# Weight tiles in a hybrid SSD and RWKV-7 step: four buffers for either part and four raw tiles while the mixer lasts, in a pool of its own

## The chip, the cores and the metric

One core of one Trainium2 chip runs the whole step. The time is device microseconds of one launch, the median of several runs. The profile comes from one profiled execution, whose own time stands beside its span below. Engines are named as in the profile: PE (matrix multiplies; PEld its weight loads), DVE, ACT, POOL, and SP, which issues nearly all DMAs.

## The reference, cut to what matters

One layer of a decoder over 576 tokens: 512 of a prompt and 8 sequences of 8 tokens with states of their own. Everything is float32.

```python
u = rmsnorm(h)
z, xbc, dt_raw, rw = jnp.split(u @ w_in, IN_SPLITS, axis=-1)     # 1024 -> 1024 + 1536 + 16 + 3328
# group A, Mamba-2 SSD, 16 heads x 64, state 128
xs, bm, cm = jnp.split(silu(conv4(xbc)), XBC_SPLITS, axis=-1)
y_ssd = ssd_norm * group_rmsnorm((ssd_chunked(xs, dt, a_head, bm, cm, ssm0) + d_skip * xs) * silu(z))
# group B, RWKV-7, 16 heads x 64
r, k, v, w_lo, a_lo, g_lo = jnp.split(rw + (prev - rw) * shift_mu, RWKV_SPLITS, axis=-1)
decay = exp(-exp(-softplus(-(w0 + tanh(w_lo) @ w2)) - 0.5)); a = sigmoid(a0 + a_lo @ a2)
gate = sigmoid(g_lo) @ g2
# per token: S = S * decay - (S kk)(kk*a)^T + v k^T ; o = S r
y_rwkv = (group_norm(o) * ln_x_w + ln_x_b + bonus) * gate
h += concat(y_ssd, y_rwkv) @ w_out                                # 2048 -> 1024
h += (silu(rmsnorm(h) @ w_gate) * (rmsnorm(h) @ w_up)) @ w_down   # 1024 -> 2816 -> 1024
h += sigmoid(rmsnorm(h) @ w_ple_gate) * (p @ w_ple_proj)
y = rmsnorm(h)
```

## The kernel before, in words

**A projection.** Activations lie channel by token: a tile is 128 channels x 576 tokens, used in two halves of 288. A float32 product is made of rounded parts: a weight block of 128x512 (four 128x128 weights) comes by one DMA of 256 KB into a tile `raw`; ACT copies it rounded into `whi`; POOL and DVE in turn subtract it, `wlo = raw - whi`. `wsplit` does these three steps (L206 the DMA, the helper `act` at L93 the copy, L213 the subtraction). The activations are split alike into `xhi` and `xlo`. For each 128x128 weight and each half `mm3` issues three matmuls: `whi` by `xhi` (L228), `whi` by `xlo` (L229), `wlo` by `xhi` (L230); a 1024-row projection of one 128-channel tile takes two blocks and 48 matmuls. Another order of the same three products, used late in the program, has line L241.

**The pool `wp`.** It lives for the whole program and holds three tiles `raw`, two `whi` and two `wlo`, 2 KB a partition each: 14 KB a partition. A tile's next user waits until the last reader of the one before is done: the DMA for `wlo` on the same `raw`, ACT's copy for the last matmul L229 on the same `whi`, the subtraction for the last matmul L230 on the same `wlo`.

**The mixer** runs until `mix.close()`, at about 680 us. RWKV's heads are worked in four quarters Q0 to Q3, each through these steps: its projections (`shifted`, L368 to L378, with the gate tiles, which need the tile `vo` made at L442 and by `split`); **prep** (L568 to L592, two passes jj0 and jj1: decay products `pb`, normalised keys `kk`, L588 and then POOL's L592, which writes half of `bk`); **gram** (L620 on PE, masked by DVE at L630 into `Lst`); a triangular **solve** on DVE (L681, L683) with round trips through DRAM; **combine** (L705 to L719); a **chain** of nine dependent steps `core` (L796, L804, L809, L819, with `prompt_state` L830 on PE and L838 on DVE); and `head_norm` (L908 on). L253 is a sum over channels behind the gram. The projections that belong to no quarter (`xbc`, `dt` and `z` tiles) are handed out between those steps and fill PE in the waits of a chain: this text calls all projection matmuls L228 to L230 the filler.

**Order.** The program is written as above, but the order on each engine is set when it is built: a scheduler goes through the written instructions with a priority for each, keeps a model of when buffers and engines come free, and puts out one list per engine. Each engine then works its list strictly in order. A change of the buffers of a pool therefore changes the lists.

**After the mixer** come the output projection, SwiGLU and the per-layer embedding, with `h` in the pool `hp` and other pools on the right side of the memory.

Of the kernel before, what the change touches and what calls it, by code (L numbers as in the profile page):

```python
# [8 lines left out]
F32 = mybir.dt.float32  # L9
F32R = mybir.dt.float32r  # L10
AF = mybir.ActivationFunctionType
ALU = mybir.AluOpType
# [4 lines left out]
P = 128  # L17
# [58 lines left out]
def hybrid_step(ctx, tc, A):  # L76
    nc = tc.nc
    V, S, G, T = nc.vector, nc.scalar, nc.gpsimd, nc.tensor

    cp = ctx.enter_context(tc.tile_pool(name="cp", bufs=1))  # L80
    wp = ctx.enter_context(tc.tile_pool(name="wp", bufs=2))
    xp = ctx.enter_context(tc.tile_pool(name="xp", bufs=8))
    lin = ctx.enter_context(tc.tile_pool(name="lin", bufs=2, space=PSUM))
    dp = ctx.enter_context(tc.tile_pool(name="dp", bufs=1, space=DRAM))
# [3 lines left out]
    def nm(s):  # L88
        uid[0] += 1
        return f"{s}_{uid[0]}"  # L90

    def act(out, in_, func=AF.Copy, scale=1.0, bias=0.0):
        return S.activation(out, in_, func, bias=bias, scale=scale)  # L93
# [80 lines left out]
    at, n = PV["shift_mu"]  # L174
    V.tensor_scalar(omu[:], pv[:, at:at + n], -1.0, 1.0, ALU.mult, ALU.add)
    hka = const("hka", [P, 16])
    at, n = PV["k_a"]
# [4 lines left out]
    flip = [0]  # L182
    only = [None]

    def below(lo, src, hi, eng):

        if eng == "D":
            act(lo, src, scale=-1.0)
            G.dma_start(lo, src, accum_op=ALU.add)
        else:  # L190
            eng.tensor_tensor(lo, src, hi.bitcast(F32), ALU.subtract)  # L191

    def split(src, pool, tags, shape, lo_eng=None, hi=None, lo=None, hi_eng=None, **kw):
# [7 lines left out]
        below(lo[:], src, hi[:], lo_eng or (G if flip[0] % 2 else V))  # L201
        return hi, lo

    def wsplit(src, n, hi=None, lo=None):
        raw = wp.tile([P, 512], F32, tag="raw", name=nm("raw"), bufs=3)
        nc.sync.dma_start(raw[:, 0:n], src)  # L206
        if hi is None:
            hi = wp.tile([P, 512], F32R, tag="whi", name=nm("whi"))
            lo = wp.tile([P, 512], F32R, tag="wlo", name=nm("wlo"))
        act(hi[:, 0:n], raw[:, 0:n])  # L210
        flip[0] += 1
        eng = only[0] or (G if flip[0] % 2 else V)
        eng.tensor_tensor(lo[:, 0:n], raw[:, 0:n], hi[:, 0:n].bitcast(F32), ALU.subtract)  # L213
        return hi, lo

    ahead = []
# [1 line left out]
    def wload(nk, hi=None, lo=None):  # L218
        if ahead:
            return ahead.pop(0)  # L220
        n = nk * P
        src = A["wts"][wat[0]:wat[0] + P * n].rearrange("(p n) -> p n", p=P)
        wat[0] += P * n
        return wsplit(src, n, hi, lo)
# [29 lines left out]


    mix = ExitStack()
    sp = mix.enter_context(tc.tile_pool(name="sp", bufs=1, side="right"))
    s2_ = ExitStack()
    s2 = s2_.enter_context(tc.tile_pool(name="s2", bufs=1, side="right"))
# [48 lines left out]
    for k in range(KT):  # L308
        hi, lo = xu[0][:, k], xu[1][:, k]
# [111 lines left out]
    def dts():  # L421
        hi, lo = wsplit(A["wdt"], P)
        ps = lin_ps()[0:16]
        for k in range(KT):
            mm3(ps, hi[:, k * 16:k * 16 + 16], lo[:, k * 16:k * 16 + 16], X[k][0], X[k][1], k == 0, k == KT - 1)
        x = cslot("dtx", [16, NT])
        act(x[:], ps, AF.Identity, bias=sm16[:, 0:1])
        e = cslot("dte", [16, NT])
        V.scalar_tensor_tensor(e[:], x[:], -1.0, x[:], ALU.mult, ALU.max)
        act(e[:], e[:], AF.Exp, scale=-1.0)  # L430
        act(e[:], e[:], AF.Ln, bias=1.0)
        V.scalar_tensor_tensor(x[:], x[:], 0.0, e[:], ALU.max, ALU.add)
        nc.sync.dma_start(dt_d[:], x[:])
# [11 lines left out]
    def gates(ugh):  # L445
        for h in range(2):
            gh, gl = wsplit(A["wg2"][:, h * 512:h * 512 + 512], 512)
            for jj in range(4):
                ps = lin_ps()
                mm3(ps, gh[:, jj * P:(jj + 1) * P], gl[:, jj * P:(jj + 1) * P], ugh[0], ugh[1], True, True)  # L450
                g = slot("g")
                act(g[:], ps)
                nc.sync.dma_start(gate_d[h * 4 + jj][:], g[:])
# [431 lines left out]
    def gate_bonus(j):  # L885
        if j < 6 and j % 2 == 0:
            gt, y = (sp.tile([P, NT], F32, tag="gt", name=nm(n), bufs=2)[:] for n in ("gt", "bvl"))
        else:
            t = pair(j // 2, "gb")
            gt, y = t[:, 0], t[:, 1]  # L890
        nc.sync.dma_start(gt, gate_d[j][:])
        nc.sync.dma_start(y, bv_d[j][:])
        return gt, y

    def head_norm(s, ahead=()):

        q = s.q
        st = tr_ps()[:, 0:20]
        Oc = []
        gsq = None if ahead else pair(q, "gsq")  # L900
        if not ahead:
            ahead = [gate_bonus(2 * q), gate_bonus(2 * q + 1)]
        for jj in jj2:
            o = s.AR[:, jj].rearrange("p g t -> p (g t)")
            sq = gsq[:, jj] if gsq else sp.tile([P, NT], F32, tag="gt", name=nm("gsq"), bufs=2)
            for a, b in HV:
                pp = cx_ps()
                marks["n", q] = T.matmul(pp[:, 0:HALF], cen[:], o[:, a:b], start=True, stop=True)  # L908
                V.tensor_copy(o[:, a:b], pp[:, 0:HALF])
                act(sq[:, a:b], pp[:, 0:HALF], AF.Square)  # L910
            token_sums(st, jj, sq)
            Oc.append(o)
        rn = inv_norm(st, "gnr", 1.0 / 64, GN_EPS)
        for jj in jj2:
            j = 2 * q + jj
            o = Oc[jj]
            gt, y = ahead[jj]
            for a, b, ps in by_channel(rn, jj, cx_ps, "rxg"):
                V.scalar_tensor_tensor(o[:, a:b], o[:, a:b], par("ln_x_w", j), ps, ALU.mult, ALU.mult)
            (V if q == 3 else G).tensor_tensor(y, y, o, ALU.add)  # L920
            yo = sp.tile([P, NT], F32, tag="gt", name=nm("yo"), bufs=2)[:] if q == 2 and jj else y
            V.scalar_tensor_tensor(yo, y, par("ln_x_b", j), gt, ALU.add, ALU.mult)
            if q < 3:
                nc.sync.dma_start(yr_d[j][:], yo)
            else:
                YR.append(split(y, xp, ("xhi", "xlo"), [P, NT], lo_eng=V))
# [357 lines left out]
    with tc.high_priority():  # L1284
        head_norm(Q[3], [gate_bonus(6), gate_bonus(7)])
    mix.close()
    hp = ctx.enter_context(tc.tile_pool(name="hp", bufs=8, side="right", reuse_waits="tile"))
    late.append(mix2.enter_context(tc.tile_pool(name="mz", bufs=1, side="right", reuse_waits="tile")))
    late.append(mix2.enter_context(tc.tile_pool(name="ps2", bufs=1, space=PSUM, reuse_waits="tile")))
# [244 lines left out]
    for a, b in ((0, 320), (320, NT)):  # L1534
        n = b - a
# [17 lines left out]
        for c in range(8):  # L1553
# [6 lines left out]
            for k in range(KT):  # L1560
                hi, lo = (w[:, k % 4 * P:k % 4 * P + P] for w in WP[c][k // 4])
# [166 lines left out]
```

## Time and profile before

| | |
|---|---|
| median of 3 runs | 1332.21 us (1329.48, 1332.21, 1340.11) |
| the profiled execution | 1330.78 us, span 1328.8 us, clock granted to PE 0.95 |
| PE / PEld | 1225.6 us (92%) / 1127.1 us (85%) |
| DVE | 887.1 us (67%) |
| ACT | 631.1 us (47%) |
| POOL | 611.6 us (46%) |
| DMA | 140.29 MB, mean 106 GB/s |

The profile's page counts each engine's busy time over the span. Its queries group instructions by line, list what each engine waited for, cut the span into windows, and print instructions one by one with the idle time ahead of them and what ended it. In a window's row stand the bounds, the length, then the busy time of PE, PEld, DVE, ACT and POOL with the number of instructions, the granted clock (PEclk, 1.00 is full), the share of DMA time and GB/s. In a row of waits stand the waiting engine, line and tile, what released it, the sum in us, the number of times and the longest. In a timeline row stand start, duration, engine, line, operation, and in brackets the idle time before it and its releaser.

### The profile page before, as it was taken

The numbers are of one execution on the slowest core, as the hardware profiler recorded it, in microseconds if no ns is written. First come the engines' busy times: TensorE is split into PE (matmuls) and PEld (weight loads), VectorE is DVE, ScalarE is ACT, GpSimd is POOL, SyncE is SP. The second block draws the span as 40 slices with busy tenths as digits, with TensorE's granted clock in tenths as the row PEclk, the third lists the DMA queues.
The fourth block names the chain that finished last, engine by engine and source line by source line (L and its number), as shares of the span: only waits on it lengthen the run. The fifth ranks groups of instructions, "written<-read, shape, count | busy, mean of one in ns | idle before, by whom it ended". The sixth has DMA issues, their size and how long they took to land. (4 is left out here: it accounts for less than half of the span.)

```text
span 1328.8 us, 26626 instructions
## 1 busy us (share of the span) xinstructions
PE 1225.6 (92%) x10429; PEld 1127.1 (85%) x10429; DVE 887.1 (67%) x1570; ACT 631.1 (47%) x1274; POOL 611.6 (46%) x583
## 2 busy tenths in 40 slices
PE   6897999999989978899989988999999999999997
PEld 5786897889968966787869868899899999999996
DVE  6648666887696886953456567868895148883464
ACT  6565436534654373343434464455553225553363
POOL 5416513642365135122455655646465345655642
PEclk9898899899978979889989989999999999999998
DMA  5322242234232313262454542253333224424322
GB/s 166 122 69 72 78 116 67 86 96 121 72 110 74 100 52 87 95 200 88 140 187 140 176 151 65 72 169 106 96 107 89 87 76 114 125 57 135 100 88 72
DMA packets 96765, 140.29 MB, mean 106 GB/s; under 512 B 34961, under 2 KB 39313, under 8 KB 96641
## 3 DMA queue, kind: packets, MB, share of 16 engines
q1 hardware_dynamic: 93760, 133.36, 32.8%
q0 software_dynamic: 2304, 4.72, 2.0%
q8 instruction: 82, 1.34, 0.4%
q10 hardware_dynamic: 576, 0.52, 0.1%
q14 instruction: 43, 0.34, 0.1%
HBM read 106.10 MB, written 27.75 MB: 101 GB/s over the span
## 5 line engine op out<-in xcount | busy, mean ns | idle before, releaser
L213 POOL TENSOR_TENSOR wlo<-raw,whi 128x512 fp32r<-128x512 f32 (+1 forms) x92 | 125.4, 1363 | 307.9 <-ACT whi L93 230.3
L228 PE MATMUL lin<-xhi,whi 128*128 128x288 f32 (+1 forms) x784 | 243.0, 311 | 2.9 <-ACT whi L93 2.1
L230 PE MATMUL lin<-xhi,wlo 128*128 128x288 f32 (+1 forms) x784 | 241.2, 308 | 2.2 <-POOL wlo L213 2.2
L229 PE MATMUL lin<-xlo,whi 128*128 128x288 f32 (+1 forms) x784 | 240.8, 307 | 0.9 <-POOL xlo L191 0.9
L93 ACT ACTIVATE whi<-raw 128x512 fp32r<-128x512 f32 (+1 forms) x200 | 123.2, 616 | 213.3 <-PE lin L241 94.9
L228 PEld LDWEIGHTS lin<-xhi,whi 128*128 128x128 f32 (+1 forms) x784 | 150.5, 192 | 9.8 <-ACT whi L93 2.6
L229 PEld LDWEIGHTS lin<-xlo,whi 128*128 128x128 f32 (+1 forms) x784 | 150.3, 192 | 6.2 <-POOL xlo L191 2.1
L230 PEld LDWEIGHTS lin<-xhi,wlo 128*128 128x128 f32 (+1 forms) x784 | 150.3, 192 | 6.0 <-POOL wlo L213 2.8
L213 DVE TENSOR_TENSOR wlo<-raw,whi 128x512 fp32r<-128x512 f32 (+1 forms) x108 | 83.5, 774 | 73.5 <-PE lin L241 37.7
L1424 PE MATMUL lin<-T,wh 128*128 128x288 f32 x576 | 87.3, 296 | 2.6 <-ACT e L93 2.2
L1424 PEld LDWEIGHTS lin<-T,wh 128*128 128x128 f32 x576 | 80.2, 190 | 3.3 <-ACT e L93 2.4
L93 ACT ACTIVATE wh<-raw 128x512 fp32r<-128x512 f32 x72 | 45.1, 629 | 53.9 <-PE lin L1424 37.1
L191 POOL TENSOR_TENSOR wl<-raw,wh 128x512 fp32r<-128x512 f32 x36 | 57.1, 1586 | 13.1 <-PE lin L1424 7.5
L191 DVE TENSOR_TENSOR wl<-sw,wh 128x512 fp32r<-128x512 f32 x54 | 50.8, 940 | 8.6 <-ACT wh L93 4.5
L241 PE MATMUL lin<-ah,whi 128*128 128x288 f32 x352 | 54.7, 294 | 0.0
L241 PE MATMUL lin<-al,whi 128*128 128x288 f32 x352 | 54.4, 295 | 0.0
L241 PE MATMUL lin<-ah,wlo 128*128 128x288 f32 x352 | 54.2, 295 | 0.0
L681 DVE TENSOR_TENSOR tmp<-L,Tt 72x30 f32<-72x30 f32 (+14 forms) x120 | 51.4, 429 | 3.2
L1424 PE MATMUL lin<-T,wl 128*128 128x288 f32 x288 | 50.2, 299 | 0.0
L241 PEld LDWEIGHTS lin<-ah,whi 128*128 128x128 f32 x352 | 49.3, 188 | 0.0
L241 PEld LDWEIGHTS lin<-al,whi 128*128 128x128 f32 x352 | 49.2, 188 | 0.0
L241 PEld LDWEIGHTS lin<-ah,wlo 128*128 128x128 f32 x352 | 49.2, 188 | 0.0
(432 smaller groups left out, 3259.2 us busy)
## 6 DMA issues: line engine op xcount, KB each, us to landing
raw<-wts SPq DMA_DIRECT2D x271, 256.0 KB, 2.6
S<-s_wkv SPq DMA_DIRECT2D x8, 512.0 KB, 5.1
hd<-s_ssm SPq DMA_DIRECT2D x8, 512.0 KB, 3.5
o_ssm_s<-hd SPq DMA_DIRECT2D x8, 512.0 KB, 2.9
xbc_d<-E SPq DMA_DIRECT2D x12, 288.0 KB, 2.1
x<-xT SPq DMA_DIRECT2D x8, 288.0 KB
gate_d<-g SPq DMA_DIRECT2D x8, 288.0 KB, 2.5
bv_d<-rw SPq DMA_DIRECT2D x8, 288.0 KB
```

Source lines behind the costliest of these rows:

```text
L93: return S.activation(out, in_, func, bias=bias, scale=scale)
L191: eng.tensor_tensor(lo, src, hi.bitcast(F32), ALU.subtract)
L213: eng.tensor_tensor(lo[:, 0:n], raw[:, 0:n], hi[:, 0:n].bitcast(F32), ALU.subtract)
L228: T.matmul(ps[:, a:b], whi, xhi[:, a:b], start=first, stop=False)
L229: T.matmul(ps[:, a:b], whi, xlo[:, a:b], start=False, stop=False)
L230: T.matmul(ps[:, a:b], wlo, xhi[:, a:b], start=False, stop=last)
L241: T.matmul(ps[:, a:e], (hi, lo)[p][:, i * P:(i + 1) * P], xs[k + i][q][:, a:e], start=n == k + i == 0, stop=n == 2 and k + i == nk - 1, sk ...
L681: V.tensor_tensor(o, L[:, jx:jx + 1, jx + 1:32].to_broadcast([NB, jx, n]), Tt[:, 0:jx, jx:jx + 1].to_broadcast([NB, jx, n]), ALU.mult)
L1424: T.matmul(ps, (hi, lo)[p][:, k * P:(k + 1) * P], OPS[n][k][q], start=first and p == q == k == 0, stop=p == 1 and k == 3, skip_group_check ...
```

## The change

`wp` is no longer opened at the start. A pool `wm` on the right side, inside the stack `mix`, serves the weight blocks until `mix.close()`, with four `raw`, four `whi` and four `wlo`: 24 KB a partition. Behind `mix.close()` a new `wp` is opened on the right side with the old numbers, three `raw` and two of either part; `reuse_waits="tile"` makes its tiles wait for the tiles that held their memory before. The subtraction goes through the helper `below`, which issues the same operation on the same engine; its line is then that helper's.

```diff
-    wp = ctx.enter_context(tc.tile_pool(name="wp", bufs=2))
...
+    wide, now = [None], [(4, 4)]
+
     def wsplit(src, n, hi=None, lo=None):
-        raw = wp.tile([P, 512], F32, tag="raw", name=nm("raw"), bufs=3)
+        pool, (nw, nr) = wide[0], now[0]
+        raw = pool.tile([P, 512], F32, tag="raw", name=nm("raw"), bufs=nr)
         nc.sync.dma_start(raw[:, 0:n], src)
         if hi is None:
-            hi = wp.tile([P, 512], F32R, tag="whi", name=nm("whi"))
-            lo = wp.tile([P, 512], F32R, tag="wlo", name=nm("wlo"))
+            hi = pool.tile([P, 512], F32R, tag="whi", name=nm("whi"), bufs=nw)
+            lo = pool.tile([P, 512], F32R, tag="wlo", name=nm("wlo"), bufs=nw)
         act(hi[:, 0:n], raw[:, 0:n])
         flip[0] += 1
-        eng = only[0] or (G if flip[0] % 2 else V)
-        eng.tensor_tensor(lo[:, 0:n], raw[:, 0:n], hi[:, 0:n].bitcast(F32), ALU.subtract)
+        below(lo[:, 0:n], raw[:, 0:n], hi[:, 0:n], only[0] or (G if flip[0] % 2 else V))
         return hi, lo
...
     mix = ExitStack()
+    wm = mix.enter_context(tc.tile_pool(name="wm", bufs=1, side="right"))
+    wide[0] = wm
     sp = mix.enter_context(tc.tile_pool(name="sp", bufs=1, side="right"))
...
     mix.close()
+    wide[0] = ctx.enter_context(tc.tile_pool(name="wp", bufs=1, side="right", reuse_waits="tile"))
+    now[0] = (2, 3)
     hp = ctx.enter_context(tc.tile_pool(name="hp", bufs=8, side="right", reuse_waits="tile"))
```

Every engine issues the same instructions as before, in another order. Three places follow. In the rows of the new program the lines are shifted (the helper `act` is L92, `below` L190, `shifted` and all behind it three lines more); numbers behind a tile's name tell its copies apart, and `x2` stands for two equal rows.

The first place is DVE at the start, in the projections of Q0. `xlo` are parts of the normalised activations, `wlo_76` is the second part of a block of Q0's fourth projection tile, and `u_68` and L442 lead to the tile `vo`. Before:

```order
L191 TENSOR_TENSOR xlo_52_442<-x_7_206,xhi_51_441 128x576
L191 TENSOR_TENSOR xlo_56_452<-x_12_216,xhi_55_451 128x576
L213 TENSOR_TENSOR wlo_76_573<-raw_74_570,whi_75_572 128x512
L368 TENSOR_TENSOR u_68_530<-lin_61_469,rstd_25_263 128x576
L191 TENSOR_TENSOR xlo_60_462<-x_14_220,xhi_59_461 128x576
L442 TENSOR_SCALAR rw_48_427<-rw_48_427 128x576
```

Now, at the same place and, some twenty rows further ahead, behind the reciprocal of the norm:

```order
L190 TENSOR_TENSOR xlo_52_442<-x_7_206,xhi_51_441 128x576
L190 TENSOR_TENSOR xlo_56_452<-x_12_216,xhi_55_451 128x576
L190 TENSOR_TENSOR wlo_92_658<-raw_90_655,whi_91_657 128x512
L371 TENSOR_TENSOR u_68_530<-lin_61_469,rstd_25_263 128x576
L190 TENSOR_TENSOR xlo_60_462<-x_14_220,xhi_59_461 128x576
L445 TENSOR_SCALAR rw_48_427<-rw_48_427 128x576
```

```order
L190 TENSOR_TENSOR wlo_67_503<-raw_65_500,whi_66_502 128x512
L347 RECIPROCAL rn5_28_276<-rn5_28_276 128x5
L190 TENSOR_TENSOR wlo_76_573<-raw_74_570,whi_75_572 128x512
L371 TENSOR_TENSOR u_30_335<-lin_29_286,rstd_25_263 128x576
L362 SCALAR_TENSOR_TENSOR x_4_200<-x_4_200,pv_66,rstd_25_263 128x576
```

`wlo_76` has moved ahead of the eight normalisations of `x` and their parts; in its old place stands `wlo_92`, the part of a later block, so that `u_68`, `xlo_60` and L442 have as much ahead of them as before.

The second place is ACT at the prep of Q0, pass jj0. `lo_160` is made of the matmuls `lin_159` and becomes the decay product `pb_163`; `E_155` and `h_156` belong to the convolution of a filler tile, `lin_146`. Before:

```order
L93 ACTIVATE sqk_145_1003<-rw_78_602,pv_69 128x576
L93 ACTIVATE lo_160_1108<-lin_159_1101,hw_113 128x576
L93 ACTIVATE lo_160_1108<-lo_160_1108,eps_t_87 128x576
L93 ACTIVATE whi_151_1048<-raw_150_1046 128x512
L93 ACT_TABLE_LOAD
L93 ACTIVATE rn_158_1097<-cb_143_990 128x20
L93 ACT_TABLE_LOAD
L93 ACTIVATE lo_162_1118<-lin_161_1111,hw_113 128x576
L93 ACTIVATE pb_163_1121<-lo_160_1108 128x576
```

Now, from behind the same `rn_158`:

```order
L92 ACTIVATE whi_195_1296<-raw_194_1294 128x512
L92 ACTIVATE E_155_1079<-lin_146_1015 128x512
L92 ACTIVATE E_155_1079<-lin_146_1015 128x8x8
L92 ACT_TABLE_LOAD
L92 ACTIVATE lo_160_1108<-lin_159_1101,hw_110 128x576
L92 ACTIVATE suv_224_1669<-tr_223_1666 64x4x64 x2
L92 ACTIVATE suv_222_1663<-tr_223_1666 64x4x64 x2
L92 ACTIVATE h_156_1087<-E_155_1079,hw_110 128x600
L92 ACTIVATE lo_160_1108<-lo_160_1108,eps_t_84 128x576
L92 ACTIVATE lo_162_1118<-lin_161_1111,hw_110 128x576
L92 ACTIVATE whi_198_1326<-raw_197_1324 128x512
L92 ACTIVATE pb_163_1121<-lo_160_1108 128x576
```

The first step of `lo_160` has gone behind two weight copies, `E_155` and the tables; on PE `lin_159` stands behind all 48 matmuls of `lin_146`, where it stood behind two of them.

The third place is PE at the end of Q2's chain: `cx_802`, `cx_808`, `cx_811` are its last steps, L908 is its `head_norm`, and `lin_948` is the last tile of the `z` filler. Before:

```order
L228 MATMUL lin_948_6471<-xhi_59_461,whi_953_6504 128x288
L229 MATMUL lin_948_6471<-xlo_60_462,whi_953_6504 128x288
L230 MATMUL lin_948_6471<-xhi_59_461,wlo_954_6505 128x288
L819 MATMUL cx_802_5417<-G_646_4409,suv_788_5347 64x64
L830 MATMUL cx_805_5430<-suv_788_5347,bkt_798_5404 64x64 x4
L819 MATMUL cx_802_5417<-G_646_4409,suv_788_5347 64x64 x3
L796 MATMUL cx_808_5449<-suv_804_5427,G_646_4409 128x128 x2
L804 MATMUL cx_810_5455<-xs_809_5452,TT0_465 64x64 x4
L809 MATMUL cx_811_5460<-ar_645_4408,suv_804_5427 64x64 x4
L819 MATMUL cx_811_5460<-G_646_4409,suv_804_5427 64x64
L830 MATMUL cx_812_5467<-suv_804_5427,bkt_807_5447 64x64 x4
L819 MATMUL cx_811_5460<-G_646_4409,suv_804_5427 64x64 x3
```

Now:

```order
L231 MATMUL lin_948_6471<-xhi_36_355,wlo_951_6475 128x288
L229 MATMUL lin_948_6471<-xhi_36_355,whi_950_6474 128x288
L799 MATMUL cx_808_5449<-suv_804_5427,G_646_4409 128x128
L230 MATMUL lin_948_6471<-xlo_37_356,whi_950_6474 128x288
L799 MATMUL cx_808_5449<-suv_804_5427,G_646_4409 128x128
L231 MATMUL lin_948_6471<-xhi_36_355,wlo_951_6475 128x288
L229 MATMUL lin_948_6471<-xhi_38_360,whi_950_6474 128x288
```

Before, all 48 matmuls of `lin_948` stood ahead of `cx_808`; now 38 of them stand behind its first matmul and are spread up to the end of `cx_811`. From L908 on the order of PE is again the same in both, up to the first matmuls behind the mixer.

## The prediction

> **What bounds the kernel now.** First the page, for the engines' shares:
>
> ```profile
> PE 1225.6 (92%) x10429; PEld 1127.1 (85%) x10429; DVE 887.1 (67%) x1570; ACT 631.1 (47%) x1274; POOL 611.6 (46%) x583
> ```
>
> PE is the bound, and the same 10429 matmuls stay. So the time can move only by PE's idle time and by the stretches in which PE has a low clock. The chain that ended last begins at 935.87 us, behind the mixer, and so can't price this change. I therefore cut the span into windows at the stages' bounds:
>
> ```profile
> 0.00:51.00 51.00, 33.37 (x216) 30.93 (x217) 40.09 (x55) 30.33 (x52) 28.57 (x50) 0.94 0.38 124
> 51.00:90.00 39.00, 37.81 (x273) 36.36 (x272) 13.00 (x27) 19.27 (x38) 6.79 (x6) 1.00 0.42 136
> 90.00:118.00 28.00, 24.38 (x195) 22.68 (x193) 21.35 (x30) 21.63 (x36) 12.80 (x19) 0.94 0.18 54
> 118.00:144.00 26.00, 15.94 (x142) 13.16 (x143) 16.75 (x26) 11.61 (x25) 20.72 (x25) 0.66 0.25 69
> 144.00:247.00 103.00, 98.81 (x878) 88.57 (x878) 75.12 (x151) 51.93 (x104) 31.97 (x40) 0.97 0.33 96
> ...
> 378.00:421.00 43.00, 35.21 (x342) 28.96 (x343) 30.73 (x66) 22.57 (x56) 25.33 (x33) 0.75 0.28 85
> ...
> 474.00:526.00 52.00, 40.76 (x515) 30.15 (x515) 40.03 (x75) 29.07 (x69) 28.41 (x33) 0.87 0.19 55
> 526.00:545.00 19.00, 19.00 (x163) 17.45 (x164) 14.71 (x42) 6.69 (x16) 3.30 (x7) 1.00 0.44 136
> 545.00:571.00 26.00, 21.92 (x170) 17.73 (x168) 21.18 (x55) 7.19 (x16) 3.89 (x4) 0.74 0.24 75
> ```
>
> Where filler stands PE is full: 98.81 of 103 us while Q0's chain runs, 19.00 of 19 at 526. It starves where filler has run out: 118 to 144 (gram of Q0, 15.94 of 26 us, clock 0.66), 378 to 421 (gram of Q2), 474 to 526 (Q3), 545 to 571 (end of Q2's chain, clock 0.74). The question is whether more weight buffers help there, so the waits come next:
>
> ```profile
> ACT whi L93 <- PE lin L229: 76.9, 50, 4.3
> POOL wlo L213 <- ACT whi L93: 230.3, 49, 19.4
> SPq L206 <- POOL wlo L213: 242.5, 74, 24.2
> SPq L206 <- DVE wlo L213: 225.7, 82, 9.7
> PE lin L230 <- DVE wlo L213: 5.4, 1, 5.4
> PE lin L230 <- POOL wlo L213: 4.7, 4, 2.4
> PE lin L228 <- ACT whi L93: 2.1, 2, 1.7
> ```
>
> By the first four rows the buffers look scarce: the weight DMA's queue waited 468 us for subtractions, ACT 76.9 us for a free `whi`. But these engines wait for PE, which is the bound. What PE itself waited for weights is in the last three rows, 12.2 us in the whole program; the longest of POOL's, 2.4 us, is at the very first block, which no buffer helps. I am left with 9.8 us, 5.4 of it in one wait, 4.4 in five short ones.
>
> The Trainium skill, "Perfetto Trace Analysis", Optimization Strategy, says that a gap repeated on the engine that should be saturated can mean too few buffers for the next tile. By that rule this change is the remedy; the rows show such a gap on ACT fifty times, on PE seven times, so I keep the rule's reading as the rival A below.
>
> **The change part by part.** *The copies themselves* cost nothing new: instructions, sizes and engines are those of before. What moves is order.
>
> *The 5.45 us wait at the start.* PE and what stood behind it:
>
> ```profile
> 40.06 0.29 PE L229 MATMUL lin<-xu,whi 128*128 128x288 f32 x1
> 45.80 0.61 PE L230 MATMUL lin<-xu,wlo 128*128 128x288 f32 x1 [5.45 <-DVE wlo L213]
> ...
> 51.24 0.30 PE L228 MATMUL lin<-vo,whi 128*128 128x288 f32 x1
> 45.06 0.68 DVE L213 TENSOR_TENSOR wlo<-raw,whi 128x512 fp32r<-128x512 f32 x1
> 47.56 1.53 DVE L442 TENSOR_SCALAR rw<-rw 128x576 f32<-128x576 f32 x1
> 49.12 0.68 ACT L93 ACTIVATE vo<-rw 128x576 fp32r<-128x576 f32 x1 [1.70 <-DVE rw L442]
> 49.88 1.47 POOL L191 TENSOR_TENSOR vo<-rw,vo 128x576 fp32r<-128x576 f32 x1 [1.11 <-ACT vo L93]
> ```
>
> `wlo_76` at 45.06 goes ahead of 21 rows of DVE, so this wait goes. The 22 matmuls left of that tile took from 45.80 to 51.24 (5.4 us); 0.247 each, where the window of full clock above, 51 to 90, has 273 in 37.81 us, 0.138 each. At that pace they take 3 us and end at about 43.3. What is late next is `vo`: the gate tiles are next on PE and need L442, ACT's copy and POOL's subtraction, which ends at 51.35. On DVE `wlo_92` has the old place of `wlo_76`, so L442 stays at 47.56. PE then idles from 43.3 to 51.3 instead of 40.3 to 45.8. **Value 0**; at best the stall and the slow clock behind it go, −8 us (5.45 and 2.4); at worst the slow clock lands on the next 22 matmuls, +2.4.
>
> *The short waits.* One lies in a stretch with filler:
>
> ```profile
> 232.20 0.61 PE L230 MATMUL lin<-xhi,wlo 128*128 128x288 f32 x1 [1.09 <-POOL wlo L213]
> ```
>
> I take **−1** for it (0 to −1.1). The other 3.3 us come before 118 us. They go too, but filler runs out before the gram: what PE saves there it waits at 118 to 144, where prep decides. **0**, with −3.3 at best.
>
> *Prep of Q0.*
>
> ```profile
> 88.35 0.72 ACT L93 ACTIVATE lo<-lin,hw 128x576 f32<-128x576 f32 x1
> 94.12 0.68 ACT L93 ACTIVATE pb<-lo 128x576 f32<-128x576 f32 x1
> 90.07 1.33 PE L503 MATMUL cb<-blk,sqk 128*64 128x2 f32 x40
> 100.98 0.83 DVE L402 SCALAR_TENSOR_TENSOR h<-E,hw,h 128x600 f32<-128x600 f32 x1
> 123.50 0.76 DVE L588 TENSOR_TENSOR lo<-lo,rw 128x576 f32<-128x576 f32 x1
> 124.28 4.64 DVE L402 SCALAR_TENSOR_TENSOR h<-E,hw,h 128x600 f32<-128x600 f32 x3
> 124.34 3.94 POOL L592 TENSOR_TENSOR bk<-lo,lo 64x576 f32<-64x576 f32 x2 [0.90 <-DVE lo L588]
> 92.00:99.00 7.00, 4.55 (x34) 4.13 (x33) 3.06 (x9) 6.85 (x13) 1.41 (x5) 1.00 0.13 37
> ```
>
> `lin_159` goes behind 46 more matmuls of filler (6.3 us at 0.138) and the 1.33 us of L503, so ACT's `lo` comes some 7.5 us after 88.35. From `lo` to `pb` took 5.8 us; in the new list these are `lo`, four `suv`, `h`, `lo`, `lo`, `whi`, about 5.3 us by their durations. So `pb` is 7 us later; of the 7 us from 92 to 99 DVE was idle for 3.9 (last row, a window), so pass jj0 ends some 3 us later. In pass jj1 three L402 of a filler tile, which ran behind L588 at 124.28, now stand ahead of it. They delay L588, then POOL's L592, whose 3.94 us end at 128.28, and the gram's last pairs. Price: 3 × 0.83 = 2.5 us as L402 runs alone, 4.64 as it ran beside L592. Nothing covers it: no filler is left in this stretch in either program. I take **+3** (nearer to the single L402, since L592 can't run beside it any more); bounds 0, if the masks on DVE end last anyway, whose work ahead is the same to 0.2 us, and +7, if the delay of `pb` passes through whole.
>
> The Trainium skill, "SBUF — State Buffer", Who interferes with whom, says that a DVE instruction with two inputs in that memory contends with a GpSimd instruction that reads there. By it L402 takes its 0.83 us once it stands ahead of L592, and this term is +2.5; by the row as it stands it is +4.6.
>
> *The grams of Q1 to Q3.* Chain steps of the quarter before move forward in the lists, filler back. Summing the trace's durations of what stands ahead of a gram's last `Lst` on DVE gives +2.0, +2.9 and +2.3 us for Q1, Q2, Q3. In return up to 107 filler matmuls (14 us) that stood ahead of Q1's chain steps now stand behind them and are there when a step waits. I take **+1** for the three together, between −4 (Q2's gram gets back half of its 7.8 idle us) and +7.2 (all three sums on the path).
>
> *The end of Q2's chain.* Before, its last steps have no filler:
>
> ```profile
> 552.56 0.45 PE L830 MATMUL cx<-suv,bkt 128*64 128x64 f32 x8 [0.47 <-DVE suv L812]
> 556.09 0.95 PE L796 MATMUL cx<-suv,G 128*128 128x128 f32 x4 [2.85 <-DVE suv L838]
> 557.40 1.04 PE L804 MATMUL cx<-xs,TT 64*64 64x64 f32 x7 [0.36 <-ACT xs L93]
> 560.85 1.81 PE L908 MATMUL cx<-ar,cen 128*128 128x288 f32 x3 [0.37 <-ACT ar L93]
> ```
>
> These gaps are 4.05 us, and the clock of 0.74 over 26 us is a half clock over some 13.6 us, which costs up to 6.8. Now 38 matmuls (5.2 us at 0.138) stand between `cx_808` and L908, while the step waits. The filler must be done anyway, so the gain is the idle time that it covers: about 4, and part of the slow clock. **−5**; bounds 0 (the steps wait on DVE, which is 21.18 of 26 us busy here with Q3's solve) and −10.
>
> *The border at `mix.close()`.* The first blocks of the new `wp` must wait for old tiles; their DMAs now wait for the last matmuls of the last partial output projection, where they went out at 657 to 667.
>
> ```profile
> 679.81 0.29 PE L230 MATMUL lin<-xhi,wlo 128*128 128x288 f32 x1
> 688.88 0.68 PE L228 MATMUL lin<-xhi,whi 128*128 128x288 f32 x2
> raw<-wts SPq DMA_DIRECT2D x271, 256.0 KB, 2.6
> ```
>
> Those matmuls end at about 680.1; a block needs 2.6 us to land, then a copy and a subtraction like those of `vo` above (0.68 and 1.47 us), so it stands ready near 685, 4 us ahead of its first matmul at 688.88. **0**; up to +3, if SP's other transfers there hold it back.
>
> **Sum.** 0 + 0 − 1 + 3 + 1 − 5 + 0 = −2. The profiled execution took 1330.78 us (span 1328.8), so 1328.8; the median of the runs, 1332.21, is 1.4 higher, and I say **1329**.
>
> **The rivals.** *A, the filler reaches the holes.* The waits were the buffers' doing, and what is saved stays saved, because the blocks that are ready early let PE run on filler while a chain waits. Price: −9.8 for the waits, −2.4 for the slow clock behind the long one, −5 at Q2's end, no loss at prep: −17, **1314**. For it: 468 us of waiting in SP's queue. Against it: 118 to 144 and 474 to 526 lack filler, not weights, and `vo` is not weight work.
>
> *B, slower: the filler's side work gets in front of prep.* Blocks that may be prepared earlier also let copies, subtractions and convolutions stand ahead of the steps that make `bk`. Place: DVE ahead of L588 in each prep. Price: +7 at Q0, and 2.0, 2.9 and 2.3 at the other three, 14.2; with no gain at Q2's end, **1345**. It decides if the second L588 starts later than about 128 us, 4.6 behind 123.50: the gram of Q0 then ends later by more than the gains give back. For it: DVE is busy 21.35 of the 28 us from 90 to 118 and ACT 21.63, more than over the whole span. Against it: 16.75 of 26 in the next.
>
> *C, it does nothing.* The waits only move from SP and ACT to somewhere else, and Q2's end is paced by DVE: **1331**.
>
> **How the numbers follow.** Forecast 0.41, A 0.23, B 0.20, C 0.16. A change of about 1% (13 us) is what a measurement of this kernel can tell from none. The forecast's terms reach from about −10 to +9, mostly inside that; faster by over 1%: A's 0.23 and a little of the forecast, 0.25; slower: 0.20; the rest, 0.55. The range has to take in A and most of B, with the terms' bounds around A: **1310 to 1347**.
>
> **What would show it.** In the changed kernel: no wait of PE for a `wlo` at 40 us, but a gap before the first `lin<-vo` that ends at about 51; the second L588 of Q0 at about 126.5 and the gram's end (L253) 3 us later than 138.3 to 143.4; L796 of Q2's last step without its 2.85 us wait, the clock in that stretch above 0.74; the time from L908 on to the end unchanged. I am wrong if the `vo` chain came earlier, if the chain steps of Q1 and Q2 run markedly faster with filler behind them, or if the blocks at the border reach PE late.

## The result, and the profile after

The changed kernel took 1345.21 us (median of 9 runs, 1340.03 to 1346.92), the kernel before 1334.82 in 9 runs beside it (1329.48 to 1343.16): **1.007 times as long, 95% interval 1.0043 to 1.0097**, 6 to 13 us slower. The profiled execution took 1340.03 us (span 1337.9), 9.25 more than the one of before; it is the fastest of the nine, and the one of before lies 4 us below its median. The page of the changed kernel, its waits, and windows at the same stages (the bounds shifted with the stages):

```profile
PE 1232.2 (92%) x10429; PEld 1137.1 (85%) x10429; DVE 882.6 (66%) x1570; ACT 633.3 (47%) x1274; POOL 606.6 (45%) x583
...
ACT whi L92 <- PE lin L230: 77.0, 48, 4.7
POOL wlo L190 <- ACT whi L92: 263.7, 56, 20.1
SPq L208 <- POOL wlo L190: 240.3, 70, 24.2
SPq L208 <- DVE wlo L190: 219.2, 80, 9.4
PE lin L229 <- ACT vo L92: 7.0, 1, 7.0
PE lin L231 <- POOL wlo L190: 2.1, 1, 2.1
```

```profile
51.00:92.00 41.00, 39.72 (x278) 38.78 (x279) 14.27 (x29) 19.40 (x38) 9.19 (x7) 0.93 0.44 135
118.00:149.00 31.00, 22.81 (x181) 19.07 (x180) 19.27 (x31) 13.73 (x29) 22.92 (x31) 0.66 0.22 59
247.00:280.00 33.00, 28.24 (x308) 23.58 (x309) 22.59 (x47) 19.09 (x48) 20.64 (x29) 0.79 0.16 36
571.00:690.00 119.00, 109.34 (x1013) 91.13 (x1012) 52.59 (x127) 51.58 (x116) 40.18 (x38) 0.94 0.43 138
690.00:818.00 128.00, 117.10 (x1030) 102.74 (x1031) 87.88 (x144) 59.35 (x138) 73.91 (x60) 0.92 0.46 151
```

The buffers did what they could: of PE's 12.2 us of waits for weights one of 2.1 is left, at the first block. In its place stands a wait of 7.0 us for `vo`. ACT still waits 77 us for a free `whi`, and SP 459.5 us for subtractions (468.2 before): with more buffers these engines still end up waiting for PE.

Where the 9 us arose shows best in the start of the same matmul in both traces. The first column is before, in us; the others are later (+) or earlier, one profiled execution each. A row named "behind" a stage is the first filler matmul after it on PE; the last row is the measured ratio of the times, each to runs of the kernel before taken beside that run.

| place | before | changed | place | raw4 | parts4 | early1 | late1 | keep4 | ord01 | fp | hold2 | hold4 | hold5 |
|---|---|---|---|---|---|---|---|---|---|---|---|---|---|
| behind the gate tiles | 59.60 | +2.0 | +0.2 | −0.3 | +3.6 | +3.0 | +0.2 | +3.6 | −0.4 | +1.8 | +0.2 | −0.5 | +0.1 |
| behind Q0's gram | 143.39 | +5.0 | +0.1 | +0.5 | +6.6 | +6.6 | +2.5 | +6.7 | +4.1 | +4.4 | +0.4 | +0.7 | +0.2 |
| behind Q1's gram | 269.44 | +10.2 | +0.3 | +1.9 | +11.8 | +7.8 | +8.4 | +15.2 | +8.5 | +7.4 | +0.7 | +4.3 | +0.2 |
| behind Q2's gram | 411.26 | +11.3 | +0.5 | +2.2 | +12.8 | +7.5 | +12.8 | +18.0 | +6.7 | +8.7 | +0.7 | +4.7 | +0.4 |
| behind Q3's gram | 526.18 | +9.0 | +0.8 | +1.8 | +11.9 | +6.8 | +8.8 | +22.8 | +13.1 | +12.7 | +2.3 | +8.0 | +0.7 |
| behind Q2's head_norm | 566.39 | +3.7 | −1.1 | +1.4 | +8.0 | +9.4 | +7.0 | +25.3 | +13.2 | +13.8 | +4.4 | +8.4 | +3.4 |
| Q3's chain, step 1 | 589.41 | +8.1 | −0.7 | +1.6 | +10.4 | +10.3 | +7.7 | +24.8 | +13.8 | +15.8 | +4.5 | +9.6 | +3.9 |
| last output projection of the mixer | 668.45 | +8.0 | −0.9 | +1.4 | +13.6 | +9.6 | +7.1 | +24.7 | +13.0 | +15.3 | +4.2 | +9.1 | +2.9 |
| behind the SSD steps | 819.46 | +8.6 | +12.5 | +8.7 | +10.9 | +17.1 | +14.5 | +26.8 | +22.3 | +15.6 | +7.7 | +14.3 | +1.1 |
| median, ratio to before | | 1.0070 | 1.0065 | 1.0066 | 1.0054 | 1.0096 | 1.0131 | 1.0181 | 1.0147 | 1.0106 | 1.0040 | 1.0063 | 1.0013 |

How far a single execution can be trusted shows in place, raw4, hold2, hold4 and hold5, whose PE lists are those of before up to about 540 us: at 526 us place, raw4, hold2 and hold5 differ from it by 0.7 to 2.3 us, and hold4 by 8.0 (4.7 at 411). A step in one column says little; a step that comes in each kernel with the same list says more.

The changed kernel's column is the account: +2.0 at the start, +3.0 in Q0, +5.3 in Q1, +1.0 in Q2, −7.5 up to Q2's `head_norm`, +4.3 from there to Q3's chain, and +0.6 behind the mixer.

### The profile page after: what moved, and what is told of

It is laid out like the page before. It is cut to its first block, busy times and chain, and to the rows that moved or that the text cites. A ratio compares the mean times of both kernels' runs of the same rounds, so it can differ in the third digit from the quotient of the medians.

```text
span 1337.9 us, 26630 instructions
## 1 busy us (share of the span) xinstructions
PE 1232.2 (92%) x10429; PEld 1137.1 (85%) x10429; DVE 882.6 (66%) x1570; ACT 633.3 (47%) x1274; POOL 606.6 (45%) x583
## 5 line engine op out<-in xcount | busy, mean ns | idle before, releaser
L190 POOL TENSOR_TENSOR wlo<-raw,whi 128x512 fp32r<-128x512 f32 (+1 forms) x92 | 122.5, 1332 | 307.7 <-ACT whi L92 263.7
L229 PE MATMUL lin<-xhi,whi 128*128 128x288 f32 (+1 forms) x784 | 246.0, 315 | 9.6 <-ACT lo L92 6.0
L92 ACT ACTIVATE whi<-raw 128x512 fp32r<-128x512 f32 (+1 forms) x200 | 123.1, 617 | 212.4 <-PE lin L242 104.1
L190 DVE TENSOR_TENSOR wlo<-raw,whi 128x512 fp32r<-128x512 f32 (+1 forms) x108 | 80.4, 744 | 70.1 <-PE lin L242 38.2
L92 ACT ACTIVATE wh<-raw 128x512 fp32r<-128x512 f32 x72 | 45.0, 628 | 52.7 <-PE lin L1429 37.2
L190 POOL TENSOR_TENSOR wl<-raw,wh 128x512 fp32r<-128x512 f32 x36 | 57.0, 1584 | 12.7 <-PE lin L1429 6.5
L190 DVE TENSOR_TENSOR wl<-sw,wh 128x512 fp32r<-128x512 f32 x54 | 49.7, 920 | 7.9 <-PE lin L1429 5.0
L686 DVE TENSOR_TENSOR Tt<-Tt,tmp 72x30 f32<-72x30 f32 (+14 forms) x120 | 49.5, 413 | 3.2
```

Of the source, the lines that this page charges most:

```text
L229: T.matmul(ps[:, a:b], whi, xhi[:, a:b], start=first, stop=False)
L686: V.tensor_tensor(Tt[:, 0:jx, jx + 1:32], Tt[:, 0:jx, jx + 1:32], o, ALU.subtract)
```

## The experiments

Theory O: deeper parts let filler tiles stand whole ahead of prep's small matmuls, and the grams come late. Its rivals: P, the pool's new place and border; D, the deeper queue of weight DMAs.

**place**, the pool as in the change with the old numbers:

```diff
-    wide, now = [None], [(4, 4)]
+    wide, now = [None], [(2, 3)]
```

> The pool moved to the right side and opened again behind the mixer, but with the old numbers (three raw, two of either part). On PE, DVE, ACT and POOL the lists up to the end of the mixer are those of before. Theory O (the loss comes from the order that the deeper parts give: filler ahead of the prep of Q0 and Q1): the time of before, within 3 us (ratio 0.998 to 1.002), and Q1's first filler behind its gram at about 269 us as before. Rival P (the place in memory and the new pool's waits at the border cost): 5 to 9 us slower, all of it behind 675 us.

Measured: 1.0065 (1.0035 to 1.0095). O's total falls, and P's place is right: nothing up to 668 us, then all of the loss. The window and the longest wait of PE there:

```profile
780.00:820.00 40.00, 30.52 (x223) 25.23 (x224) 21.35 (x28) 22.84 (x55) 18.69 (x15) 0.74 0.32 105
782.63 1.89 PE L1163 MATMUL d<-cd,hd 128*64 128x8 f32 x32 [3.57 <-DMA hd<-s_ssm]
```

In the same window of before PE was busy 31.95 us at a clock of 0.94. This wait is not the whole of it: raw4, with the same order there, doesn't wait for this load and loses as much time. So the changed kernel's +0.6 behind the mixer doesn't mean that the border is free; two losses of like size, one in the mixer and one behind it, come and go apart.

**raw4** (`now = [(2, 4)]`):

> As place, but four raw tiles and two of either part: only SP's list differs from place. Theory O: the time of place, within 2 us. Rival D (more weight DMAs in the queue stand ahead of the solve's round trips): 3 to 6 us slower, with L705's wait for Ad or Td longer than 1.0 us in each quarter.

1.0066 (1.004 to 1.0093), as place. D falls, with one wait for `AA<-Ad` above 1.0 us (1.8) instead of four: the fourth raw tile neither gains nor costs what could be measured.

**parts4** (`now = [(4, 3)]`):

> As the changed kernel, but three raw tiles instead of four: four of either part. PE's list differs from the changed kernel's in ten places only. Theory O: the time of the changed kernel, 1.005 to 1.009 of before, with the same +5 us at Q0's L253 and +10 at Q1's. Rival D: back to before, 0.998 to 1.002.

1.0054 (1.0027 to 1.0081), with the changed kernel's steps at the start, Q0 and Q1 and nothing lost behind the mixer. What the change does in the mixer is the work of the parts.

**early1** and **late1** keep the moved pool and three raw tiles. They give the weight parts two tags of two buffers each and use the second tag in a part of the program only (early1: until Q0's chain is written; late1: from Q1 on). The lines are late1's; early1 begins with `True` and sets `False` at this place:

```diff
+            pick[0] = 1 - pick[0] if deep[0] else 0
+            hi = pool.tile([P, 512], F32R, tag=f"whi{pick[0]}", name=nm("whi"), bufs=nw)
...
+        if s.q == 1:
+            deep[0] = True
         fill_for(s)
         prep(s)
```

> Four buffers for either part until the chain of Q0 is written, then two of the same four; three raw tiles. Theory O: the start and Q0 as in the changed kernel (+2 at the gate tiles, +5 at Q0's L253), Q1 nearly as before, so +4 to +6 us in all (1.003 to 1.0045). If Q0's lateness is caught up later by slack in the chain, which no row of the changed kernel shows, 0 to +2.

> The changed kernel, but with two of the four parts until the chain of Q0 is written and four from Q1 on; three raw tiles. Theory O: gate tiles and L253 of Q0 as before (within 1 us), L253 of Q1 +3 to +6, and the end of Q2's chain nearly without the changed kernel's gain (10 matmuls behind its last step instead of 38). 668.5 us late by 3 to 8.

early1 took 1.0096 (1.006 to 1.0131), more than expected: it is 9.6 us late at the end of the mixer already, where 4 to 6 in all were expected, and loses 7.5 more behind it. late1 took 1.0131 (1.0098 to 1.0165), with 7.1 at the end of the mixer as expected and 7.4 behind it. Up to Q1's gram they split the loss: early1 has the start and Q0 and then +1.2 in Q1, late1 nothing at the start, +2.3 in Q0 (unexpected) and +5.9 in Q1. Against its expectation late1 also gains 5.7 us between Q2's gram and Q2's `head_norm`, though it has few matmuls behind the chain's last step.

**keep4** leaves the pool of before in its place and takes two more buffers of either part from a second pool while the mixer lasts:

```diff
+            turns[0] += 1
+            pool = more[0] if more[0] and turns[0] % 2 == 0 else wp
+            hi = pool.tile([P, 512], F32R, tag="whi", name=nm("whi"), bufs=2)
...
     mix = ExitStack()
+    wm = mix.enter_context(tc.tile_pool(name="wm", bufs=2, side="right"))
+    more[0] = wm
```

> The pool of before stays where it is for the whole program; while the mixer lasts every second block takes its two parts from two more buffers of either part on the right side (four of either part in all, three raw tiles), and nothing is opened anew behind the mixer. Theory O, narrowed after the run place (the deeper parts delay the mixer by their order; what the border and the SSD steps behind it do is another matter): the last output projection of the mixer (before at 668.5 us) 6 to 11 us late, L253 of Q0 about +5 and of Q1 about +9; the stretch from there to 820 us as long as before within 3 us; in all +6 to +12 us. Rival P2 (only the moved pool costs, the mixer's lateness is caught up): 668.5 us may be late, but the end at most +3 us.

1.0181 (1.0147 to 1.0216): +24.7 at the end of the mixer, far above the 6 to 11, then +2.1. Without any new pool at the border four parts lose most of all, so the mixer's lateness is not caught up and P2 falls. Why its Q3 loses so much more than the changed kernel's is open.

**ord01** has the buffers of before; only lora's matmuls in Q0 and Q1 are queued behind the filler tile written ahead of them (`tail[0]` is that tile's last matmul). Lora is the name for prep's products that make `lo` (`lin_159` is the first), 24 matmuls a quarter:

```diff
+            with tc.issue_after(tail[0].ins) if q < 2 else nullcontext():
+                mm3(ps, wl[0][:, c], wl[1][:, c], UL[0], UL[1], True, True)
```

> The kernel of before with its buffers; only the small matmuls of prep (lora) in Q0 and Q1 are queued behind the filler tile that is written ahead of them, as the changed kernel's list has them. Theory O: this displacement alone makes L253 of Q0 2 to 4 us late and L253 of Q1 4 to 8 us in all, with the start untouched; 668.5 us late by 3 to 8. Rival W (lateness comes from the weight copies and subtractions that run early, not from the place of lora): 0 to +1 at both.

1.0147 (1.0108 to 1.0187). L253 of Q0 is 3.3 us late, of Q1 7.7, the end of the mixer 13. Its rows, DVE and PE at Q0's gram, beside the changed kernel's (L591 and L592 are before's L588):

```profile
128.26 0.75 DVE L592 TENSOR_TENSOR lo<-lo,rw 128x576 f32<-128x576 f32 x1
131.07 1.22 PE L624 MATMUL lin<-G,bk 64*128 64x128 f32 x4 [4.30 <-POOL bk L596]
```

```profile
130.43 0.76 DVE L591 TENSOR_TENSOR lo<-lo,rw 128x576 f32<-128x576 f32 x1
131.27 3.24 POOL L595 TENSOR_TENSOR bk<-lo,lo 64x576 f32<-64x576 f32 x2 [6.10 <-DVE lo L591]
133.10 1.22 PE L623 MATMUL lin<-G,bk 64*128 64x128 f32 x4 [2.94 <-POOL bk L595]
```

With old buffers and no other edit the place of these small matmuls makes both grams about as late as in the changed kernel (+3.0 and +5.3 there without the start, +4.1 and +4.3 here). W, by which the place costs nothing, falls. The end of the mixer, 13 us late, is beyond the 3 to 8 expected.

**fp** is the changed kernel with prep's filler tiles written behind the first lora products:

```diff
-FP = ((1, 0, 1, 0, 1, 0, 0, 0), (1, 0, 1, 0, 1, 0, 0, 0), (1, 0, 1, 0, 1, 0, 0, 0), (0, 0, 0, 0, 0, 0, 0, 3))
+FP = ((0, 1, 0, 1, 1, 0, 0, 0), (0, 1, 0, 1, 1, 0, 0, 0), (0, 1, 0, 1, 1, 0, 0, 0), (0, 0, 0, 0, 0, 0, 0, 3))
```

> The changed kernel, with the filler tiles of the preps of Q0, Q1 and Q2 written one place later, behind the first two lora products. Theory O: L253 of Q0 at +0 to +3 of before instead of +5, of Q1 at +1 to +5 instead of +10, and 668.5 us at least 4 us earlier than in the changed kernel. If the lateness comes from the weight work running early, both stay at +5 and +10.

Behind Q0's gram it is +4.4 instead of +5.0, behind Q1's +7.4 instead of +10.2: O's direction, but outside O's ranges (Q0's gain is 0.6, Q1's 2.2). The end of the mixer is 15.3 late, not 4 us earlier than the changed kernel's, and the time 1.0106 (1.0067 to 1.0144): Q3's gram loses 4 us more, and the changed kernel's gain up to Q2's `head_norm` doesn't come.

How far fp undid the displacement can be counted in the traces. The filler matmuls ahead of lora's first and last products are 434 and 504 in Q0 and 984 and 1032 in Q1 before; 480 and 528, 1008 and 1056 in the changed kernel and in ord01; 432 and 480, 960 and 1008 in fp. So in fp lora stands no later than before, and still Q0 loses 2.6 us and Q1 3.0, where the changed kernel's lost 3.0 and 5.3. In Q0 the lateness comes in further on: `lo` starts at 89.95 us, 1.6 late like the start, but the second half of `kk` is 5.4 us late (97.3 before), behind a subtraction that waited for its copy and a convolution step of the filler:

```profile
100.44 1.34 DVE L190 TENSOR_TENSOR wlo<-raw,whi 128x512 fp32r<-128x512 f32 x1 [1.52 <-ACT whi L92]
101.96 0.84 DVE L405 SCALAR_TENSOR_TENSOR h<-E,hw,h 128x600 f32<-128x600 f32 x1 [0.18 <-ACT h L92]
102.72 0.34 DVE L584 SCALAR_TENSOR_TENSOR kk<-rw,pv,cb 128x128 f32<-128x128 f32 x1
```

So lora's place is enough to make a gram late, by ord01, but it is not the only way: the filler's side work ahead of `kk` does it too. What share either has in the changed kernel is not shown.

**hold2, hold4, hold5**: the kernel of before; the last 36, 24 or 18 matmuls of `lin_948` are queued behind the first step of Q2's last chain step (`HOLD` 2, 4, 5):

```diff
+                with tc.issue_after(hold[0].ins) if hold[0] and k + i >= HOLD else nullcontext():
+                    mm3(ps, hi[:, i * P:(i + 1) * P], lo[:, i * P:(i + 1) * P], xh, xl, k + i == 0, k + i == nk - 1)
...
+        if s.q == 3:
+            fill(2)
+            hold[0] = marks[2, 8]
+            fill(1)
+            hold[0] = None
```

> The kernel of before with its buffers; only the last 36 matmuls of the last z tile (lin_948) are queued behind the first step of Q2's last chain step, as the deeper buffers did with 38. Q0 and Q1 stay as they were, and the SSD steps behind the border keep nearly the order of before (filler ahead of r_1246: 2688 as before). Theory G (the changed kernel's gain at Q2's end was real and was lost because Q3's solve, late from the earlier grams, held Q3's combine): L908 of Q2 4 to 6 us early, L705 of Q3 (before at 581.8) 3 to 6 us early too, since the solve is on time, and the end 3 to 6 us early: 0.995 to 0.998. Rival H (combine of Q3 can't come earlier than about 580 us whatever PE does, as its solve on DVE sets it): L908 early, L705 at most 2 us early, the end within 2 us of before.

> As hold2, but the last 24 matmuls of lin_948 are held. Up to the border the same gain within 2 us (24 matmuls are 3.3 us), but the order of the SSD steps comes out as in the runs place, early1 and ord01 (2714 filler matmuls ahead of r_1246 instead of 2688). Theory K (that order costs 8 to 10 us between 668 and 820 us): the end 4 to 8 us later than before. Rival: those 8 to 10 us came from the new pool or from lateness in the mixer, and this run ends 2 to 4 us early.

> As hold2, but the last 18 matmuls of lin_948 are held, and the order of the SSD steps comes out as in the changed kernel (2705 filler matmuls ahead of r_1246). Theory K: 0 to +4 us between 668 and 820 us, as the changed kernel had about +1, so the end within 3 us of before.

hold2 took 1.004 (1.002 to 1.0059), hold4 1.0063 (1.0043 to 1.0082), hold5 1.0013 (0.9993 to 1.0033). G and H both miss: from 526 to 566 us the three are 2.1, 0.4 and 2.7 us later, and none is earlier at Q2's end. In hold2 the wait of 2.85 us at L796 is gone, and PE's waits are now these:

```profile
551.31 0.58 PE L805 MATMUL cx<-xs,TT 64*64 64x64 f32 x5 [2.79 <-DVE xs L800]
565.12 1.24 PE L909 MATMUL cx<-ar,cen 128*128 128x288 f32 x4 [1.10 <-DVE so L839]
567.56 0.59 PE L504 MATMUL tr<-blk,gsq 128*64 128x2 f32 x8 [1.20 <-ACT gsq L93]
```

The filler that covers the last step was taken from the step before it, which waits instead.

K, by which the order of the SSD steps sets what is lost behind the mixer, has the times right: hold4 is 7 us slower, hold5 2. In the stretch itself it misses, with 5.2 us for hold4 instead of 8 to 10 and −1.8 for hold5 instead of 0 to 4. Here are, for each kernel, the number of filler matmuls ahead of the SSD step `r_1246` (at 717.72 us before) in the lists, and what the stretch from 668.45 to 819.46 us lost: changed 2705, +0.6; parts4 2705, −2.7; fp 2704, +0.3; hold5 2705, −1.8; against 2712 or 2714 in place (+13.4), raw4 (+7.3), early1 (+7.5), late1 (+7.4), keep4 (+2.1), ord01 (+9.3), hold4 (+5.2). hold2, with before's 2688, lost 3.5 all the same. ord01 and hold4 have no new pool and lose 9.3 and 5.2, so the loss doesn't need it. It goes with the order, though not strictly (keep4 and hold2 stand across); that it is this displacement which causes it was not tried by itself.

## Why the prediction was wrong, step by step

The sum was −2, measured +9 in the profiles; the range held the time, the sign did not. Of the 11 us between, 5.3 come from Q1 to Q3 (6.3 up to Q2's gram, +1 forecast), 2 from the start, 1.8 from Q2's end, 1 from the short waits and 0.6 from behind the mixer.

- **The start (0).** The wait for `wlo` went and the one for `vo` came, as the step said. But the value was near its bound of +2.4, and L442 (now L445) did not stay at 47.56:

```profile
48.91 1.51 DVE L445 TENSOR_SCALAR rw<-rw 128x576 f32<-128x576 f32 x1
51.19 0.85 PE L229 MATMUL lin<-vo,whi 128*128 128x288 f32 x2 [6.97 <-ACT vo L92]
53.00 0.61 PE L230 MATMUL lin<-vo,whi 128*128 128x288 f32 x1 [0.96 <-POOL vo L190]
53.65 0.44 PE L229 MATMUL lin<-vo,whi 128*128 128x288 f32 x1
51.20:58.00 6.80, 5.84 (x26) 5.31 (x27) 3.62 (x7) 3.23 (x7) 1.73 (x1) 0.61 0.43 155
```

  Behind 7 us of waiting the gate tiles ran at the slow pace (clock 0.61 from 51.2 to 58), where before they had nearly the full clock (0.98 from 51 to 58). Their 48 matmuls spread over 2.05 us more; 0.37 of it are longer waits, among them one of 0.96 for the second part of `vo`, and 1.7 the slow pace. All five kernels with four parts at the start show +1.8 to +3.6, all seven without −0.5 to +0.2. The Trainium skill, "TensorE: Matmul & The Clock Gate", Part 1, has the clock halved after an idle window of about 3.4 us until as long a busy one has passed; the rows agree, with 6.97 us of waiting and then about 5 us of slow matmuls (0.24 us apart instead of 0.13, up to 56.5). Moving a wait from ahead of one tile to ahead of the next moves the slow stretch along.
- **Prep of Q0 (+3).** Right in size: +3.0 without the start. But the price was worked out for another way, so the size was partly luck. ACT's `lo` came 9.1 us late (7.5 expected) and `pb` 8.6:

```profile
97.47 0.74 ACT L92 ACTIVATE lo<-lin,hw 128x576 f32<-128x576 f32 x1
102.74 0.69 ACT L92 ACTIVATE pb<-lo 128x576 f32<-128x576 f32 x1 [0.23 <-DVE lo L571]
125.03 0.35 DVE L584 SCALAR_TENSOR_TENSOR kk<-rw,pv,cb 128x128 f32<-128x128 f32 x1 [1.56 <-PE cb L536]
125.29 0.84 DVE L405 SCALAR_TENSOR_TENSOR h<-E,hw,h 128x600 f32<-128x600 f32 x1
126.71 0.83 DVE L405 SCALAR_TENSOR_TENSOR h<-E,hw,h 128x600 f32<-128x600 f32 x1
128.14 0.83 DVE L405 SCALAR_TENSOR_TENSOR h<-E,hw,h 128x600 f32<-128x600 f32 x1
```

  In pass jj1 `kk` at 125.03 was 6.7 us late already, and the three convolution steps behind it add 0.3 us to L588 (130.43, 6.9 late). They ran at 0.83 each, as one alone did before, not at 4.64 for three. So the lateness came down from `lo` and `pb`, the way that the text had only as its upper bound; 2 us of it are the start's. That L588 would start later than 128 was the text's own mark for rival B.
- **Q1 to Q3 (+1): the step that failed.** Q1 alone lost 5.3, where the text gave +1 to three quarters. Its prep had the displacement of Q0's, filler ahead of lora, which the text had worked out for Q0; for Q1 it counted only DVE's work ahead of the last `Lst` (+2.0) and then set nearly all of that against a hoped-for cover. L588 of Q1's second pass shows it:

```profile
248.94 1.75 DVE L588 TENSOR_TENSOR lo<-lo,rw 128x576 f32<-128x576 f32 x1
...
259.38 0.76 DVE L591 TENSOR_TENSOR lo<-lo,rw 128x576 f32<-128x576 f32 x1
```

  The first row is before's, the second the changed kernel's, 10.4 us later. ord01 shows that lora's place alone can cost as much; fp, with lora put forward again, still loses 3.0 us there, so what of the 5.3 us is lora's place and what the filler's other work ahead of prep stays open.
- **Q2's end (−5).** From Q2's gram on the changed kernel gained 7.5 us up to `head_norm`; L796 lost its wait, and the clock from 545 to 567 us was 0.96. But waits of 0.99 and 2.44 us came behind it:

```profile
561.44 0.45 PE L833 MATMUL cx<-suv,bkt 128*64 128x64 f32 x8 [0.99 <-DVE suv L815]
564.57 1.78 PE L911 MATMUL cx<-ar,cen 128*128 128x288 f32 x4 [2.44 <-DVE so L841]
```

  and hold2 shows that 36 of such matmuls alone bring nothing. The gain goes with Q1's last chain steps: the last but one, at 433.93 us before, comes at 420.28 now, amid Q2's gram, though that gram is 11 us later. In the changed kernel, parts4 and late1 Q1's `head_norm` is 8 to 10 us early, and these three alone gain more than 2 us between Q2's gram and Q2's `head_norm` (4.8 to 7.5); this was not isolated. And 4.3 us of it were given back up to Q3's chain, which the text did not have as a term. Rows of before, then of the changed kernel: the solve's end on DVE, the last load of its result, and L705, L708 now:

```profile
566.68 1.06 DVE L684 COPY L<-Tt 36x1024 f32<-36x1024 f32 x1
572.22 0.50 SPq L697 DMA_DIRECT2D AA<-Ad  x1
581.75 1.92 PE L705 MATMUL cx<-AA,Lst 32*32 32x32 f32 x64
```

```profile
577.11 0.28 DVE L516 RECIPROCAL gnr<-gnr 128x20 f32<-128x20 f32 x1 [2.78 <-ACT gnr L92]
581.70 1.04 DVE L687 COPY L<-Tt 36x1024 f32<-36x1024 f32 x1
586.96 0.50 SPq L700 DMA_DIRECT2D AA<-Ad  x1
589.30 1.91 PE L708 MATMUL cx<-AA,Lst 32*32 32x32 f32 x62 [1.11 <-DMA AA<-Ad]
```

  Such a load lands some 2.2 us after its start, so before the solve's result lay ready about 7 us ahead of combine. Now the solve ends 15.0 us later, 9 by the late gram and 6 more, most of them (4.9) where its last steps on DVE stand among those of `head_norm`, one of which (L516) waits 2.78 us for ACT. Combine waits 0.94 and 1.11 us for the load; the other 2.3 us were lost ahead of it and in L708 to L722, and no run took them apart. Here the late gram cost twice: at once, and where its solve came due. The time from L908 on, which the text expected unchanged, grew from 768.0 to 773.3 us.
- **Short waits and border (−1 and 0).** The waits went; nothing of them is seen in the sum. The border's 0 became +0.6, but place shows that 0 was luck: the same pool with old parts loses 13 us behind it in its profile and 0.65% in time. The text had looked at the first blocks' DMAs there and not at the order of the SSD steps.
- **The rivals.** B named the direction, the mechanism (filler's work ahead of prep) and the mark; its 1345 is the median measured. That agreement is partly luck: it stood for +14, the medians taken side by side differ by 10.4, and those of before came out 2.6 higher than in the first three runs. It had 0.20 because its price was thought to need every quarter on the path, while two quarters, the start and the late solve made most of it up.

## What to carry to other kernels

Where a scheduler orders the work, more buffers are a change of order first: list what stands ahead of the small steps that a later wait hangs on, in every repetition of the stage, and price each one in full before setting gains against it. A gain on an engine that waits for a chain must be followed to the next place where something else comes due; here a solve on another engine had about 7 us of slack and lost it. And split a change that moves a pool and deepens it: here the move alone cost about what the whole did, and the deeper parts without the move (keep4) more.

## What the runs showed that was not expected

The effects don't add: the pool moved alone loses 0.65%, four parts in it 0.54%, four parts without moving it 1.8%. Every one of the eleven kernels tried was slower than before or the same (1.0013 to 1.0181), though some of the edits name only 18 (hold5), 36 (hold2) or 48 (ord01) of the 10429 matmuls. And two profiled executions with the same list on PE up to that point, hold4 and hold2, were 4.0 us apart at 411 us and 5.7 at 526, so a step of that size needs more than one kernel to be believed.
